# Dilated attention scores of a decoder trunk: from float32 products to float32r parts

## The chip, the cores and the metric

The kernel runs on one core of a Trainium2 chip. The metric is device time in microseconds (us) of one execution, the median of several runs. TensorE (PE in the profile; PEld is its weight load), VectorE (DVE), ScalarE (ACT) and GpSimd (POOL) each work through a queue of their own, in the order in which the program was built; SyncE (SP) issues the transfers. A semaphore makes an instruction at the head of a queue wait for another engine, and everything behind it in that queue waits too.

## The reference, cut to what matters

Two layers; each is a half-step SwiGLU, a token mixing and another half-step SwiGLU, all with residual and layer norm, on 256 tokens of width 1024 in float32. The mixing has 4 MLA heads, 6 dilated heads and 6 NSA heads. The change is in the scores of the dilated heads:

```python
def dilated_attention(q, k, v):
    for window, dil in DIL_PATTERNS:            # (128, 1), (512, 4), (2048, 16)
        o, lse = banded_attention(to_sub(q), to_sub(k), to_sub(v), window // dil)
    ...
    w = jax.nn.softmax(jnp.stack(lses, axis=-1), axis=-1)
    return jnp.einsum('bshp,pbshd->bshd', w, jnp.stack(outs))

o_b = dilated_attention(apply_rope(heads(dq), cos, sin), apply_rope(heads(dk), cos, sin), heads(dv))
```

On 256 tokens the three patterns are one softmax over the causal keys in which every key carries a weight of 0 to 3 (how many patterns reach it), and this is how the kernel computes it.

## The kernel before

Weights are streamed from memory in tiles of 128 x 1024 (`wst`, five buffers). ACT writes a float32r part `wh` of each (L76) and DVE the remainder `wl` (L77); tiles of the next stage's first weights are called `exh` and `exl`. A product of activations and weights is three float32r matmuls (`mm3`, L103 to L105): high by high, high by low, low by high. `ph`, `acc`, `pj` and `acco` are their results in PSUM: SwiGLU in, SwiGLU out, projections of the mixing, and the output projection.

The mixing is written in the order: project `a`, `b`, `nq`, `ks`; MLA; `compressed`; `nsa(0)`; project `dq` and rotate it; `nsa(1)`; project `dk` and rotate it; project `dv`; `dilated(0)`, `dilated(1)`; output projection; layer norm. The index is the block of 128 query tokens. The build's scheduler turns this into one queue for each engine and mixes the stages, so that matmuls of a later stage stand between those of an earlier one.

One unit of attention (`probs`) is: mask and scores on PE into `sc` (L460, L465), row maximum on DVE (L469), exponentials on ACT (L475 for NSA, L477 with a multiplication by the key's weight on DVE, L478, for dilated heads), reciprocal and normalisation on DVE (L480, L486), four transposes on PE into the single PSUM bank `pt` (L490), and a copy to `pT` on ACT (L492). `nsa(1)` has six units. When all units of a block are done, `weigh` multiplies them with the values into `ov` (L502), and `heads_out` (L507 on ACT, L508 on DVE) writes the heads that the output projection reads.

The output projection has 96 matmuls `acco` in a layer, and its eight blocks of heads are taken in the order `O_ORDER = (0, 1, 5, 6, 7, 2, 3, 4)`. Blocks 0 and 1 are MLA, 5 to 7 NSA, 2 to 4 dilated. So 24 matmuls need MLA alone, 18 need `nsa(0)`, 18 need `nsa(1)`, 18 `dilated(0)` and 18 `dilated(1)`: 42 of the 96 can run before `nsa(1)` has ended.

Rotated queries and keys are transposed on PE into the PSUM bank `ptr`, of which there is one (L440). For the dilated heads the copies out of it were, for each block, one of ACT for the queries (L765) and two of ACT for the keys (L773), the latter into a tile with zeros that POOL had set (L769), so that one float32 matmul gives the scores of two heads. The NSA scores already work in float32r parts: queries `nqS` hold the rounded half in partitions 0 to 63 and its remainder in 64 to 127, and keys `ksH`, `ksL` hold each part twice, so that two matmuls give all four products.

Of the kernel before, what the change touches and what calls it, by code (L numbers as in the profile page):

```python
# [49 lines left out]
def trunk(ctx: ExitStack, tc: tile.TileContext, a: dict):  # L50
    nc = tc.nc
# [141 lines left out]
    def cview(c, t, n):  # L193
        return con[:, c + t * n:c + (t + 1) * n]
# [144 lines left out]
    def mixing(l):  # L339
        with tc.tile_pool(name="apool", bufs=1, reuse_waits="tile") as ap_:  # L340
            widths = {"rt1": 384, "rt2": 384, "rq": 384, "qmT": 1024, "kmT": 1536, "wuq": 768, "cT": 768, "pr": 512}

            def new(shape, name, bufs=1, tag=None, dt=F32):

                if tag is None:
                    return ap_.tile(shape, dt, tag=name, name=name, bufs=bufs)
                m = math.prod(shape[1:])
                v = ap_.tile([P, widths.get(tag, 384)], F32, tag=tag, name=name, bufs=bufs)[:shape[0], :m]
                if len(shape) == 3:
                    v = v.rearrange("p (a b) -> p a b", a=shape[1])  # L350
                if len(shape) == 4:
                    v = v.rearrange("p (a b c) -> p a b c", a=shape[1], b=shape[2])
                return v
# [40 lines left out]
            cT = new([P, 3, S], "cT", 1, "cT")  # L394
# [41 lines left out]
            def transposed(src, n, w=P):  # L436

                pv = bank("ptr").rearrange("p (k s) -> p k s", k=4)
                for k in range(n):
                    nc.tensor.transpose(pv[:w, k], src[:, k * w:(k + 1) * w], ident)  # L440
                return pv[:w, :n]

            def rotated(ps, t, H):
                r = new([P, 384], "rq", 2, "rq")
                rope(r[:, :H * 64].rearrange("p (h n) -> p h n", h=H),
                     ps[t][:, :H * 64].rearrange("p (h n) -> p h n", h=H),
                     cview(C_COS, t, 64), cview(C_SIN, t, 64), H, 32)
                return transposed(r, H // 2)
# [69 lines left out]
            for t in range(2):  # L518
# [5 lines left out]
                                     scale=float(128 ** -0.5), accum_out=ss[:, 1:2])  # L524
# [9 lines left out]
                                        in1=gain[:, :, None].to_broadcast([P, 3, P]), op=OP.mult)  # L534
# [4 lines left out]
            qmT = new([96, 4, S], "qmT", 1, "qmT")  # L539
            kmT = new([96, 4, S], "kmT", 1, "kmT")  # L540
            for t in range(2):
                tsl = slice(t * P, (t + 1) * P)
# [24 lines left out]
            for v in range(2):  # L567
                for g in range(2):
                    for par in range(2):
                        src = kcT[g * 64:(g + 1) * 64, v, :].rearrange("p (c j r) -> p j r c", j=8, r=2)  # L570
                        for half in range(2):

                            rows = slice(8 * half, 8 * half + 8)
                            nc.vector.tensor_tensor(
                                out=E[par * 64:(par + 1) * 64, v, rows, g * 16:g * 16 + 15],
                                in0=src[:, :, par, half:half + 15],
                                in1=posT[par * 64:(par + 1) * 64, v, rows, None].to_broadcast([64, 8, 15]),
                                op=OP.add)
# [131 lines left out]
            def dilated(t):  # L710
                tsl = slice(t * P, (t + 1) * P)
                nk = (t + 1) * P
                ov = ov_tile()
                order = in_order()
                neg = tri if t == 0 else dilm
                mult = con[:, C_MULT + 256 - nk:C_MULT + 256]
                pT = {}
                for js in ((0, 1), (2,)) if t == 0 else ((0,), (1,), (2,)):
                    w = probs(t, [(dqT[:, j, tsl], [dkT[:, j, :, :nk]], 2) for j in js], nk, neg, mult=mult)
                    for i, j in enumerate(js):  # L720
                        pT[j] = w[:, 2 * i * (t + 1):2 * (i + 1) * (t + 1)]
# [12 lines left out]
            nqS = new([P, 2, 3, S], "nqS", dt=F32R)  # L734
            ksH = new([P, 2, 2, S], "ksH", dt=F32R)
            ksL = new([P, 2, 2, S], "ksL", dt=F32R)
            for t in range(2):
                tsl = slice(t * P, (t + 1) * P)
                raw = new([P, 384], "raw", 2, "rq")
                nc.scalar.activation(raw, pn[t][:, :384], AF.Copy)  # L740
                nc.scalar.activation(nqT[:, :, tsl], transposed(raw, 3), AF.Copy, scale=0.125)
                pv = rotated(pn, t, 6)
                for g in range(2):
                    top = nqS[0:64, g, :, tsl]
                    nc.scalar.activation(top, pv[g * 64:(g + 1) * 64], AF.Copy, scale=0.125)  # L745
                    nc.vector.scalar_tensor_tensor(out=nqS[64:128, g, :, tsl], in0=pv[g * 64:(g + 1) * 64], scalar=0.125,
                                                   in1=top.bitcast(F32), op0=OP.mult, op1=OP.subtract)
            mla(0)
            pk_, = project("ks")
            mla(1)  # L750
            for t in range(2):
                tsl = slice(t * P, (t + 1) * P)
                pv = rotated(pk_, t, 4)
                for g in range(2):
                    for half in range(2):
                        hi = ksH[half * 64:(half + 1) * 64, g, :, tsl]
                        nc.scalar.activation(hi, pv[g * 64:(g + 1) * 64], AF.Copy)
                        nc.vector.tensor_tensor(out=ksL[half * 64:(half + 1) * 64, g, :, tsl],
                                                in0=pv[g * 64:(g + 1) * 64], in1=hi.bitcast(F32), op=OP.subtract)
            pTc = [compressed(t) for t in range(2)]  # L760
            nsa(0, pTc[0])
            pdq, = project("dq")
            dqT = new([P, 3, S], "dqT", 1, "qmT")
            for t in range(2):
                nc.scalar.activation(dqT[:, :, t * P:(t + 1) * P], rotated(pdq, t, 6), AF.Copy, scale=0.125)  # L765
            nsa(1, pTc[1])
            pdk, = project("dk")
            dkT = new([P, 3, 2, S], "dkT", 1, "kmT")
            nc.gpsimd.memset(dkT, 0.0)  # L769
            for t in range(2):  # L770
                pv = rotated(pdk, t, 6)
                for g in range(2):
                    nc.scalar.activation(dkT[g * 64:(g + 1) * 64, :, g, t * P:(t + 1) * P],  # L773
                                         pv[g * 64:(g + 1) * 64], AF.Copy)
            pdv, = project("dv")
            vd = [new([P, 6, 64], f"vd{t}", 1, f"qm{t}") for t in range(2)]
            for t in range(2):
# [150 lines left out]
```

## Time and profile before

| | before |
|---|---|
| median of 3 runs | 1044.63 us (1043.99 to 1044.65) |
| profiled execution | 1045.1 us |
| its span in the trace | 1042.4 us |
| mean granted TensorE clock | 0.999 |
| PE busy | 1028.8 us (99%) |
| DVE busy | 666.8 us (64%) |
| ACT busy | 509.0 us (49%) |

The span runs from the first to the last instruction; the 2.7 us between it and the execution's time lie around the program. Busy PE time is the union of records that overlap (a matmul's record outlasts the start of the next), so 99% says that PE rarely stood with nothing in it, and what a matmul costs is read from the distance between starts, not from the length of its record. A share over the whole span says little of a stage: the mixing of layer 0 ends at 333 us, that of layer 1 at 848 us, and in these stages the other engines are far busier than on the mean.

### The profile page before, as it was taken

What the parts mean: (1) busy time and instruction counts of PE and PEld (TensorE: products, weight loads), DVE (VectorE), ACT (ScalarE), POOL (GpSimd) and SP (SyncE); (2) the same over time, 40 slices, a digit from 0 to 9 for tenths busy, and PEclk for the clock granted to TensorE, in tenths of its full rate; (3) what the DMA queues carried; (4) which work ended last, traced back from release to release, by engine and by line L of the source; (5) the groups of instructions that cost most, each with busy time, mean ns of one, the idle gap of its engine ahead of it and who ended that gap; (6) DMA issues with size and microseconds to landing.
All of it is one profiled execution on the core that took longest, in us unless ns stands there. A gap on an engine that the chain in (4) does not pass through costs nothing.

```text
span 1042.4 us, 14003 instructions
## 1 busy us (share of the span) xinstructions
PE 1028.8 (99%) x5226; PEld 841.7 (81%) x5226; DVE 666.8 (64%) x1061; ACT 509.0 (49%) x832; POOL 23.2 (2%) x35
## 2 busy tenths in 40 slices
PE   9999999999999999999999999999999999999997
PEld 6888888878877888888888888888888778888885
DVE  6655555875989555555665555567679884555554
ACT  7544444435785344444334444434358844444440
POOL 0000000100000000000000000002000000000000
PEclk9999999999999999999999999999999999999999
DMA  9866657553462555657565665567515544666541
GB/s 343 307 188 185 192 182 246 202 177 108 134 226 87 173 185 183 185 163 229 171 241 163 185 189 188 183 206 267 189 40 175 190 141 148 184 186 192 182 146 41
DMA packets 59540, 190.22 MB, mean 182 GB/s; under 512 B 7120, under 2 KB 8784, under 8 KB 58704
## 3 DMA queue, kind: packets, MB, share of 16 engines
q1 hardware_dynamic: 59184, 189.07, 56.3%
q8 instruction: 41, 0.67, 0.3%
q10 hardware_dynamic: 288, 0.26, 0.1%
q14 instruction: 27, 0.22, 0.1%
HBM read 188.26 MB, written 1.05 MB: 182 GB/s over the span
## 4 chain that ended last, share of the span: by engine, by line
PE 94%; DMA 2%; ACT 2%; DVE 1%; issue 0%; DVEq 0%; ACTq 0%; SPq 0%
PE ph L105 15%; PE ph L104 15%; PE ph L103 15%; PE acc L105 8%; PE acc L104 8%; PE acc L103 8%; PE pj L105 3%; PE pj L103 3%; PE pj L104 3%; PE ov L502 2%; PE ptg L259 2%; DMA exh<-in_w 2%; PE pt L490 2%; PE acco L103 1%; PE ptr L440 1%; PE sc L465 1%
## 5 line engine op out<-in xcount | busy, mean ns | idle before, releaser
L77 DVE TENSOR_TENSOR wl<-wst,wh 128x1024 fp32r<-128x1024 f32 (+3 forms) x316 | 352.7, 1125 | 256.8 <-ACT wh L76 254.0
L76 ACT ACTIVATE wh<-wst 128x1024 fp32r<-128x1024 f32 (+3 forms) x316 | 307.0, 979 | 284.6 <-PE ph L105 175.6
L103 PE MATMUL ph<-wh,xh 128*128 128x512 f32 x640 | 252.4, 395 | 0.0
L104 PE MATMUL ph<-wl,xh 128*128 128x512 f32 x640 | 250.0, 391 | 0.1
L105 PE MATMUL ph<-wh,xl 128*128 128x512 f32 x640 | 250.1, 391 | 0.0
L104 PEld LDWEIGHTS ph<-wl,xh 128*128 128x128 f32 x640 | 120.3, 188 | 25.0 <-DVE wl L153 0.8
L103 PEld LDWEIGHTS ph<-wh,xh 128*128 128x128 f32 x640 | 120.3, 188 | 24.8 <-ACT wh L152 0.7
L105 PEld LDWEIGHTS ph<-wh,xl 128*128 128x128 f32 x640 | 120.1, 188 | 25.0
L105 PE MATMUL acc<-wh,gl 128*128 128x512 f32 x288 | 113.5, 394 | 0.0
L103 PE MATMUL acc<-wh,gh 128*128 128x512 f32 x288 | 112.9, 392 | 0.0
L104 PE MATMUL acc<-wl,gh 128*128 128x512 f32 x288 | 112.8, 392 | 0.0
L103 PE MATMUL pj<-wh,xh 128*128 128x384 f32 (+3 forms) x224 | 77.9, 348 | 0.3
L105 PE MATMUL pj<-wh,xl 128*128 128x384 f32 (+3 forms) x224 | 78.0, 348 | 0.0
L104 PE MATMUL pj<-wl,xh 128*128 128x384 f32 (+3 forms) x224 | 77.3, 345 | 0.0
L250 ACT ACTIVATE sg<-ph 128x256 f32<-128x256 f32 x88 | 33.5, 384 | 74.4 <-PE ph L105 74.4
L104 PEld LDWEIGHTS acc<-wl,gh 128*128 128x128 f32 x288 | 54.1, 188 | 12.2
L103 PEld LDWEIGHTS acc<-wh,gh 128*128 128x128 f32 x288 | 54.1, 188 | 11.6
L105 PEld LDWEIGHTS acc<-wh,gl 128*128 128x128 f32 x288 | 54.1, 188 | 11.0
L252 DVE TENSOR_TENSOR g<-sg,ph 128x256 f32<-128x256 f32 x88 | 36.7, 421 | 34.0 <-ACT sg L250 16.6
L103 PEld LDWEIGHTS pj<-wh,xh 128*128 128x128 f32 x224 | 42.3, 189 | 2.7 <-ACT nqS L745 0.7
L104 PEld LDWEIGHTS pj<-wl,xh 128*128 128x128 f32 x224 | 42.4, 189 | 1.8
L105 PEld LDWEIGHTS pj<-wh,xl 128*128 128x128 f32 x224 | 42.3, 189 | 1.7
(175 smaller groups left out, 1165.2 us busy)
## 6 DMA issues: line engine op xcount, KB each, us to landing
wst<-in_ffin SPq DMA_DIRECT2D x156, 512.0 KB, 4.5
wst<-in_ffout SPq DMA_DIRECT2D x88, 512.0 KB, 3.6
wst<-in_ffin SPq DMA_DIRECT2D x40, 256.0 KB, 5.0
exh<-in_w SPq DMA_DIRECT2D x16, 512.0 KB, 6.2
wst<-in_w_out SPq DMA_DIRECT2D x16, 512.0 KB, 4.5
gb<-in_lngb SPq DMA_DIRECT2D x6, 1024.0 KB, 6.8
wst<-in_w_b SPq DMA_DIRECT2D x16, 256.0 KB, 5.5
wst<-in_w_nq SPq DMA_DIRECT2D x8, 384.0 KB, 4.8
```

The source lines that it names most:

```text
L76: nc.scalar.activation(h[:, c], src[:, c], AF.Copy)
L77: nc.vector.tensor_tensor(out=l[:, c], in0=src[:, c], in1=h[:, c].bitcast(F32), op=OP.subtract)
L103: nc.tensor.matmul(out, lhsT=xh, rhs=wh, start=start, stop=False)
L104: nc.tensor.matmul(out, lhsT=xh, rhs=wl, start=False, stop=False)
L105: nc.tensor.matmul(out, lhsT=xl, rhs=wh, start=False, stop=stop)
L250: nc.scalar.activation(sg, ps[:, :256], AF.Silu)
L252: nc.vector.tensor_tensor(out=g, in0=sg, in1=ps[:, 256:], op=OP.mult)
L259: nc.tensor.transpose(pt[:, k, t], gs[t][:, k * P:(k + 1) * P], ident)
L440: nc.tensor.transpose(pv[:w, k], src[:, k * w:(k + 1) * w], ident)
L465: nc.tensor.matmul(sv[:, i:i + m] if m > 1 else sv[:, i], lhsT=qT, rhs=part, start=False, stop=True, skip_group_check=True)
L490: nc.tensor.transpose(pt[:, b * P:(b + 1) * P], pr[:, b * P:(b + 1) * P], ident)
L502: order(nc.tensor.matmul(out[g * 64:(g + 1) * 64], lhsT=v, rhs=p_, start=i == 0, stop=i == n - 1, skip_group_check=True))
```

## The change

The scores of the dilated heads are computed from float32r parts, as those of NSA were. The queries become `dqS` (rounded half above its remainder, by `stacked`), the keys `dkH` and `dkL`, `dkM` (rounded part and remainder, each written to both halves of the partitions, by `twice`). The remainder of the third head of a half lies in a tile of its own, `dkM`. The tiles take the places of ended ones: `dqS` that of `kmT`, `dkH` that of `nqS`, `dkL` that of `qmT`, `dkM` that of `cT`. The memset of `dkT` goes. `stacked` and `twice` also take over the unchanged NSA steps.

```diff
+            def stacked(dst, pv, tsl):
+                for g in range(2):
+                    top = dst[0:64, g, :, tsl]
+                    nc.scalar.activation(top, pv[g * 64:(g + 1) * 64], AF.Copy, scale=0.125)
+                    nc.vector.scalar_tensor_tensor(out=dst[64:128, g, :, tsl], in0=pv[g * 64:(g + 1) * 64], scalar=0.125,
+                                                   in1=top.bitcast(F32), op0=OP.mult, op1=OP.subtract)
+            def twice(hi, lo, pv, tsl):
+                for g in range(2):
+                    for half in range(2):
+                        rows = slice(half * 64, (half + 1) * 64)
+                        top = hi[rows, g, :, tsl]
+                        nc.scalar.activation(top, pv[g * 64:(g + 1) * 64], AF.Copy)
+                        j = 0
+                        for l in lo:
+                            n = l.shape[2]
+                            nc.vector.tensor_tensor(out=l[rows, g, :, tsl], in0=pv[g * 64:(g + 1) * 64, j:j + n],
+                                                    in1=top[:, j:j + n].bitcast(F32), op=OP.subtract)
+                            j += n
...
-                    w = probs(t, [(dqT[:, j, tsl], [dkT[:, j, :, :nk]], 2) for j in js], nk, neg, mult=mult)
+                    w = probs(t, [(dqS[:, g, j, tsl], [dkH[:, g, j, :nk], dkL[j][:, g, :nk]], 1)
+                                  for j in js for g in range(2)], nk, neg, mult=mult)
...
-            dqT = new([P, 3, S], "dqT", 1, "qmT")
-            for t in range(2):
-                nc.scalar.activation(dqT[:, :, t * P:(t + 1) * P], rotated(pdq, t, 6), AF.Copy, scale=0.125)
+            dqS = new([P, 2, 3, S], "dqS", 1, "kmT", F32R)
+            for t in range(2):
+                stacked(dqS, rotated(pdq, t, 6), slice(t * P, (t + 1) * P))
             nsa(1, pTc[1])
             pdk, = project("dk")
-            dkT = new([P, 3, 2, S], "dkT", 1, "kmT")
-            nc.gpsimd.memset(dkT, 0.0)
-            for t in range(2):
-                pv = rotated(pdk, t, 6)
-                for g in range(2):
-                    nc.scalar.activation(dkT[g * 64:(g + 1) * 64, :, g, t * P:(t + 1) * P],
-                                         pv[g * 64:(g + 1) * 64], AF.Copy)
+            dkH = ap_.tile([P, 2, 3, S], F32R, tag="nqS", name="dkH", bufs=1)
+            dkL01 = new([P, 2, 2, S], "dkL", 1, "qmT", F32R)
+            dkL2 = new([P, 2, 1, S], "dkM", 1, "cT", F32R)
+            dkL = [dkL01[:, :, 0], dkL01[:, :, 1], dkL2[:, :, 0]]
+            for t in range(2):
+                twice(dkH, [dkL01, dkL2], rotated(pdk, t, 6), slice(t * P, (t + 1) * P))
```

The scheduler also lays the queues out anew. Three places are shown; those of layer 1 read the same. In the changed kernel the lines have moved: L743 and L744 are the two instructions of `stacked`, L753 and L757 those of `twice`.

**PE, from the second transposition of the rotated dilated queries into the units of `nsa(1)`.** Before, `ptr` is that transposition, `pt` are the transposes of one unit of `nsa(1)`:

```order
L440 MATMUL ptr<-ident,rq 128x128 x3
L104 MATMUL acco<-wl,oTh 128x512
L105 MATMUL acco<-wh,oTl 128x512
L103 MATMUL acco<-wh,oTh 128x512
L490 MATMUL pt<-ident,pr 128x128 x4
L104 MATMUL acco<-wl,oTh 128x512
L105 MATMUL acco<-wh,oTl 128x512
L103 MATMUL acco<-wh,oTh 128x512
L104 MATMUL acco<-wl,oTh 128x512
L490 MATMUL pt<-ident,pr 128x128 x4
L105 MATMUL acco<-wh,oTl 128x512
```

Of the changed kernel, the end of 18 `acco` that follow the second `ptr`, and all that stands from there to the products `ov` of `nsa(1)`:

```order
L104 MATMUL acco<-wl,oTh 128x512
L105 MATMUL acco<-wh,oTl 128x512
L490 MATMUL pt<-ident,pr 128x128 x8
L460 LDWEIGHTS identb
L460 MATMUL sc<-tri,identb 128x2x128
L465 MATMUL sc<-ksH,nqS 128x512
L465 MATMUL sc<-ksL,nqS 128x512
L490 MATMUL pt<-ident,pr 128x128 x4
L460 LDWEIGHTS identb
L460 MATMUL sc<-tri,identb 128x512
L490 MATMUL pt<-ident,pr 128x128 x4
L460 LDWEIGHTS identb
```

Before, 1 `acco` stands between the two `ptr`, 3 between the second and the first `pt`, and 25 between the first `pt` and `ov`. In the changed kernel these counts are 18, 18 and 0. Later, 43 stand from the end of `nsa(1)`'s `ov` to that of `dilated(1)` before, and 35 in the changed kernel.

**DVE, at the last three units of `nsa(1)`.** Before (`exl` are splits of the first weights of the SwiGLU that follows the mixing; L480, L485 and L486 end a unit):

```order
L469 TENSOR_REDUCE nm<-sc 128x2
L485 TENSOR_TENSOR rs<-rs,gates_1829 128x2
L480 RECIPROCAL rs<-rs 128x2
L486 TENSOR_TENSOR pr<-pr,rs 128x512
L485 TENSOR_TENSOR rs<-rs,gates_1829 128x2
L486 TENSOR_TENSOR pr<-pr,rs 128x512
L77 TENSOR_TENSOR wl<-wst,wh 128x1024
L480 RECIPROCAL rs<-rs 128x2
L485 TENSOR_TENSOR rs<-rs,gates_1829 128x2
L486 TENSOR_TENSOR pr<-pr,rs 128x512
L77 TENSOR_TENSOR wl<-wst,wh 128x1024
L77 TENSOR_TENSOR exl<-wst,exh 128x512 x8
```

In the changed kernel:

```order
L744 SCALAR_TENSOR_TENSOR dqS<-ptr,dqS 64x3x128
L77 TENSOR_TENSOR wl<-wst,wh 128x1024
L744 SCALAR_TENSOR_TENSOR dqS<-ptr,dqS 64x3x128
L77 TENSOR_TENSOR exl<-wst,exh 128x512 x5
L480 RECIPROCAL rs<-rs 128x2
L77 TENSOR_TENSOR exl<-wst,exh 128x512
L485 TENSOR_TENSOR rs<-rs,gates_1829 128x2
L469 TENSOR_REDUCE nm<-sc 128x2
L486 TENSOR_TENSOR pr<-pr,rs 128x512
L480 RECIPROCAL rs<-rs 128x2
L77 TENSOR_TENSOR exl<-wst,exh 128x512
L485 TENSOR_TENSOR rs<-rs,gates_1829 128x2
```

The eight splits `exl` stood behind the last unit of `nsa(1)`; five of them now stand ahead of the last three units and three between these, while the splits `wl` have moved ahead.

**DVE, from the end of `nsa(1)` into the dilated heads.** Before (`nm` is a unit's row maximum, L478 the weighting of its exponentials):

```order
L508 TENSOR_TENSOR oTl<-ov,oTh 128x384
L469 TENSOR_REDUCE nm<-sc 128x4
L469 TENSOR_REDUCE nm<-sc 128x2
L478 SCALAR_TENSOR_TENSOR pr,rs<-pr,con 128x128 x5
L480 RECIPROCAL rs<-rs 128x4
```

In the changed kernel:

```order
L508 TENSOR_TENSOR oTl<-ov,oTh 128x384
L757 TENSOR_TENSOR dkL<-ptr,dkH 64x2x128
L757 TENSOR_TENSOR dkM<-ptr,dkH 64x128
L757 TENSOR_TENSOR dkL<-ptr,dkH 64x2x128
L757 TENSOR_TENSOR dkM<-ptr,dkH 64x128
L77 TENSOR_TENSOR wl<-wst,wh 128x1024
L757 TENSOR_TENSOR dkL<-ptr,dkH 64x2x128
L757 TENSOR_TENSOR dkM<-ptr,dkH 64x128
L77 TENSOR_TENSOR wl<-wst,wh 128x1024
L757 TENSOR_TENSOR dkL<-ptr,dkH 64x2x128
L757 TENSOR_TENSOR dkM<-ptr,dkH 64x128
L77 TENSOR_TENSOR wl<-wst,wh 128x1024
```

Eight pairs of `dkL` and `dkM` now stand between the end of `nsa(1)` and the last unit of `dilated(1)`. On ACT the eight copies `dkH` (L753) stand where four copies `dkT` stood; the first of each block waits for PE's transposes, each of the other three for DVE.

## Rows read from the trace of the kernel before

**Rows 1.** The page, busy time of each engine, with its share and instructions.

```profile
PE 1028.8 (99%) x5226; PEld 841.7 (81%) x5226; DVE 666.8 (64%) x1061; ACT 509.0 (49%) x832; POOL 23.2 (2%) x35
```

**Rows 2.** Busy time by engine in stretches of both layers' mixing.

```profile
core 0: us, PE busy (x) PEld busy (x) DVE busy (x) ACT busy (x) POOL busy (x), PEclk, DMA share, GB/s
291.07:293.34 2.27, 2.27 (x15) 1.65 (x14) 2.27 (x6) 1.45 (x3) 0.00 (x0) 1.00 0.43 120
293.34:303.06 9.72, 9.72 (x55) 7.21 (x54) 9.27 (x19) 9.03 (x23) 0.00 (x0) 1.00 0.59 189
303.06:306.50 3.44, 3.44 (x61) 3.27 (x61) 3.34 (x7) 2.83 (x6) 0.00 (x0) 1.00 0.90 283
306.50:325.74 19.24, 18.74 (x96) 13.34 (x94) 16.25 (x48) 12.40 (x26) 0.00 (x0) 1.00 0.50 164
325.74:333.25 7.51, 6.92 (x50) 5.56 (x51) 6.51 (x13) 2.88 (x5) 0.93 (x1) 1.00 0.04 13
808.19:817.91 9.72, 9.72 (x56) 7.18 (x55) 9.27 (x19) 9.02 (x23) 0.00 (x0) 1.00 0.59 189
821.34:840.58 19.24, 18.74 (x96) 13.34 (x94) 16.25 (x48) 12.40 (x26) 0.00 (x0) 1.00 0.50 160
```

**Rows 3.** Timeline of PE, layer 0: start, length, instruction, idle before it.

```profile
291.07 0.55 PE L440 MATMUL ptr<-ident,rq 128*128 128x128 f32 x3
...
293.34 0.66 PE L490 MATMUL pt<-ident,pr 128*128 128x128 f32 x4
...
294.77 0.60 PE L490 MATMUL pt<-ident,pr 128*128 128x128 f32 x4
...
303.06 1.09 PE L502 MATMUL ov<-pT,vs 128*64 128x128 f32 x16
...
306.50 0.55 PE L440 MATMUL ptr<-ident,rq 128*128 128x128 f32 x3
...
325.74 1.53 PE L502 MATMUL ov<-pT,vd 128*64 128x128 f32 x24 [0.46 <-ACT pT L492]
```

**Rows 4.** The same timeline: first and last of nine `acco` in a row.

```profile
319.12 0.40 PE L105 MATMUL acco<-wh,oTl 128*128 128x512 f32 x1
...
320.99 0.40 PE L104 MATMUL acco<-wl,oTh 128*128 128x512 f32 x1
```

**Rows 5.** The same timeline: dilated scores, each float32 matmul two records, and what follows.

```profile
308.57 1.46 PE L465 MATMUL sc<-dkT,dqT 128*128 128x256 f32 x6
309.68 0.59 PE L104 MATMUL acco<-wl,oTh 128*128 128x512 f32 x1
...
311.83 1.02 PE L465 MATMUL sc<-dkT,dqT 128*128 128x512 f32 x2
312.68 0.38 PE L460 MATMUL sc<-dilm,identb 128*128 128x512 bf16 x1
```

**Rows 6.** The same timeline: first and last of three float32r scores of NSA.

```profile
270.03 0.28 PE L465 MATMUL sc<-ksL,nqS 128*128 128x256 f32 x1
...
270.26 0.28 PE L465 MATMUL sc<-ksL,nqS 128*128 128x256 f32 x1
```

**Rows 7.** Groups by line and shape: count, busy us, mean ns, idle before.

```profile
L773 ACT ACTIVATE dkT<-ptr 64x384 f32<-64x384 f32 x8 | 3.9, 486 | 1.4 <-PE ptr L440 1.3
L765 ACT ACTIVATE dqT<-ptr 128x384 f32<-128x384 f32 x4 | 2.0, 492 | 1.3 <-PE ptr L440 1.3
L746 DVE SCALAR_TENSOR_TENSOR nqS<-ptr,nqS 64x384 fp32r<-64x384 f32 x8 | 4.4, 556 | 1.7 <-ACT nqS L745 1.5
L758 DVE TENSOR_TENSOR ksL<-ptr,ksH 64x256 fp32r<-64x256 f32 x16 | 6.7, 421 | 0.6
L574 DVE TENSOR_TENSOR exl<-kcT,posT 64x120 f32<-64x120 f32 x32 | 7.9, 276 | 0.3
```

**Rows 8.** Waits, whole trace: total us, times, longest.

```profile
ACT ksH L757 <- DVE ksL L758: 2.0, 4, 0.5
```

**Rows 9.** Timeline of DVE, layer 0: the eight splits `exl`.

```profile
301.94 5.09 DVE L77 TENSOR_TENSOR exl<-wst,exh 128x512 fp32r<-128x512 f32 x8
```

**Rows 10.** Timeline of PE: the matmuls that warm it up, at the program's start.

```profile
1.19 4.45 PE L163 MATMUL warm<-zero 128*128 128x512 bf16 x10 [1.19 <-DVE zero L160]
```

More of the change, by code (lines that the diff above doesn't have):

```diff
@@ L347, in new @@
                 m = math.prod(shape[1:])
-                v = ap_.tile([P, widths.get(tag, 384)], F32, tag=tag, name=name, bufs=bufs)[:shape[0], :m]
+                v = ap_.tile([P, widths.get(tag, 384)], dt, tag=tag, name=name, bufs=bufs)[:shape[0], :m]
                 if len(shape) == 3:
@@ L741, in mixing @@
                 nc.scalar.activation(nqT[:, :, tsl], transposed(raw, 3), AF.Copy, scale=0.125)
-                pv = rotated(pn, t, 6)
-                for g in range(2):
[L744 to L747, printed above, removed]
+                stacked(nqS, rotated(pn, t, 6), tsl)
             mla(0)
@@ L752, in mixing @@
                 tsl = slice(t * P, (t + 1) * P)
[L753 to L759, printed above, removed]
+                twice(ksH, [ksL], rotated(pk_, t, 4), tsl)
             pTc = [compressed(t) for t in range(2)]
@@ L762, in mixing @@
             pdq, = project("dq")
-            dqT = new([P, 3, S], "dqT", 1, "qmT")
+            dqS = new([P, 2, 3, S], "dqS", 1, "kmT", F32R)
             for t in range(2):
-                nc.scalar.activation(dqT[:, :, t * P:(t + 1) * P], rotated(pdq, t, 6), AF.Copy, scale=0.125)
+                stacked(dqS, rotated(pdq, t, 6), slice(t * P, (t + 1) * P))
             nsa(1, pTc[1])
             pdk, = project("dk")
-            dkT = new([P, 3, 2, S], "dkT", 1, "kmT")
-            nc.gpsimd.memset(dkT, 0.0)
+            dkH = ap_.tile([P, 2, 3, S], F32R, tag="nqS", name="dkH", bufs=1)
+            dkL01 = new([P, 2, 2, S], "dkL", 1, "qmT", F32R)
+            dkL2 = new([P, 2, 1, S], "dkM", 1, "cT", F32R)
+            dkL = [dkL01[:, :, 0], dkL01[:, :, 1], dkL2[:, :, 0]]
             for t in range(2):
-                pv = rotated(pdk, t, 6)
-                for g in range(2):
-                    nc.scalar.activation(dkT[g * 64:(g + 1) * 64, :, g, t * P:(t + 1) * P],
-                                         pv[g * 64:(g + 1) * 64], AF.Copy)
+                twice(dkH, [dkL01, dkL2], rotated(pdk, t, 6), slice(t * P, (t + 1) * P))
             pdv, = project("dv")
```

## The prediction

> **What bounds the kernel now.** I read the page's shares first: PE is busy 99% of the span, DVE 64%, ACT 49% [rows 1]. By these alone PE is the bound, and each PE cycle saved is time saved. A share over a whole span hides stages, though, so I then read the stage that the change touches. I cut the end of layer 0's mixing at five points of PE's timeline [rows 3]: A, from the first transposition of the rotated dilated queries (291.07) to the first transposes of `nsa(1)` (293.34); B, from there to the first products of `nsa(1)` (303.06); the products themselves, 3.44 us; C, from the first transposition of the dilated keys (306.50) to the products of `dilated(1)` (325.74); D, from there to the SwiGLU (333.25). The busy times of these stretches [rows 2] are to be read across: PE is full, but in B DVE is busy 9.27 and ACT 9.03 of 9.72 us, and in C DVE 16.25 of 19.24. Here three engines are nearly full at once. PE is full only because matmuls of the output projection stand between the steps of the softmax units, 25 of them in B and 43 in C. Layer 1 shows the same lengths, 9.72 and 19.24 [rows 2], so every sum below counts twice.
>
> **The matmuls themselves.** Before, three float32 matmuls of 256 columns take 1.11 us (308.57 to 309.68) and one of 512 takes 0.85 (311.83 to 312.68) [rows 5]: in a layer 1.11 + 3 x 0.85 = 3.7 us. Now there are 12 float32r matmuls of 128 columns and 12 of 256. Those of 256 stand 0.23 / 2 = 0.12 apart for NSA [rows 6], so 1.4 us. No row has one of 128 columns. Below, half of 0.12 bounds it (0.06); above, half of a 256-column float32 matmul (1.11 / 3 / 2 = 0.19). I take 0.11, near the row of the same type, since each still loads 128 columns of weights: 12 x 0.11 = 1.3. So PE saves 3.7 - 2.7 = 1.0 us in a layer, 1.6 or 0.0 at the bounds. This is a gain only where PE sets the pace.
>
> **Stage A, the moved matmuls.** The queue decides. Before, 4 `acco` stand between the first `ptr` and the first `pt` of `nsa(1)`; now 18 + 18 = 36. PE takes its matmuls in order, and one `acco` costs (320.99 - 319.12) / 8 = 0.234 us [rows 4]. The units of `nsa(1)` therefore start 32 x 0.234 = 7.5 us later. Moving work forward on a full engine is free as long as what it leaves behind stays full; that is the question of B. Inside A the new query steps are hidden: for each block ACT does two copies of about 0.49 where it did one of 0.49, and DVE adds two of 0.556 [rows 7], 3.2 us on both engines together in a layer, under 36 x 0.234 = 8.4 us of matmuls. They must alternate (copy, remainder, copy, remainder) before the bank is free for the second `ptr`: 2 x (0.49 + 0.556) = 2.1 us and whatever else stands between them in the two queues; the 18 `acco` there cover 18 x 0.234 = 4.2. If that cover were gone, A would be longer by what exceeds it, at most a few tenths.
>
> **Stage B, the units without cover.** All 42 `acco` that don't need `nsa(1)` are now used up ahead of it, and none stands in B. What is left for PE there is six groups of transposes and three scores. The units wait for ACT and DVE: the bank `pt` is single, so a unit's transposes wait for the copy of the previous one. Two neighbours without exponentials between them stood 1.43 us apart (293.34 to 294.77) [rows 3]; six such rounds are 8.6 us, the lower bound. The exponentials of the last three units stand behind the first copies in ACT's queue, now as before, so these units can't have run ahead during A. On DVE, splits `exl` of 5.09 / 8 = 0.64 us [rows 9] stand among the units where `wl` stood. As a chain of the same length on the same engines I keep B at 9.7 us: 0, or -1.1 at the lower bound. PE's 25 x 0.234 = 5.9 us of cover are gone and B is no shorter, so the 7.5 us of A are lost whole.
>
> **Stage C, the keys.** Before, four copies of 0.486 on ACT brought the keys in. Now there are eight, and sixteen remainders on DVE: 64 x 256 at 0.421, and 64 x 128, which no row has, at the 0.276 of 64 x 120 [rows 7]. That is 8 x 0.697 = 5.6 us on DVE, which was busy 16.25 in C and keeps its units and its three splits `wl` there: 21.8 us. This alone is more than the 19.24 that C took. Besides, each copy after a block's first waits for DVE's remainders. NSA's keys do that now, and the trace shows the wait [rows 8]. In the first steps DVE has nothing else in its queue, so it idles for two copies and their handover, 2 x 0.6 = 1.2 us. C becomes 21.8 + 1.2 = 23.0 us: +3.8. Lower bound +2.6 (no idling). Upper bound: the eight steps, 0.486 + 0.697 each, lie wholly in the chain where four copies lay, 9.5 - 1.9 = +7.6. I take +3.8, since the units of `dilated(0)` and the splits can fill the gaps of the second block. The 1.0 us saved on PE lies in this stage, where DVE now sets the end; it buys nothing. D keeps its work (19 `acco` instead of 18): 0. The memset was on POOL, busy 2% [rows 1]; no engine waits for it: 0.
>
> **The sum.** 7.5 + 0 + 3.8 = 11.3 us in a layer, 22.6 in two. The profiled execution took 1045.1 us, so 1067.7; the median of the runs lies 0.5 lower, so I predict 1067 us, 2.2% more.
>
> **Rivals.** (1) *PE sets the end everywhere*: the shares say so [rows 1], and PE had no idle time in A, B and most of C. Then only its work counts, 2 x 1.0 us less: 1043 us, or between 1041 and 1045 at the bounds of the 128-column price. It needs B to shrink by the full 7.5 us, that is to 2.2, and C not to grow; the two break even when B and C together give back 7.5 us in a layer. Against it: DVE's 9.27 of 9.72 and six rounds of 1.43. Chance 0.07, of which 0.04 faster by over 0.2% (about what a measurement of this kernel can tell from no change) and 0.03 within it. (2) *The units are cheaper without neighbours*: B falls to 8.6 and the keys hide behind the units in C: 7.5 - 1.1 = 6.4 a layer, 1058 us. For it speaks DVE's 3 us of idle time in C. Chance 0.10. (3) *The keys go through in single file*: 7.5 + 7.6 = 15.1 a layer, 1075 us. For it: the bank `ptr` is single, so the second block's transposition waits for the first block's last remainder. Chance 0.10. (4) *The clock falls* while PE waits in B and C. In every stretch read here the granted clock is 1.00, the 2.4 GHz level [rows 2], but in none does PE wait as much as it now would. At the program's start 512 columns took 4.45 / 10 = 0.445 us [rows 10] instead of 0.234; the 54 `acco` after B at that price would add 54 x 0.21 = 11.4 us a layer: 1090 us. The Trainium skill ("TensorE: Matmul & The Clock Gate", Part 1) says that the low level is the default and that activity releases it, which speaks for this rival; no stretch of this trace shows a fall after waiting. PE keeps working about half of B in short pieces, so I give it 0.04.
>
> **How the numbers follow.** The forecast, A and C both paid, has 0.69; its own range, from B and C at their bounds, is 1063 to 1075. With rivals (2) and (3) the range 1057 to 1077 holds about 0.89; what is left out is the clock and rival (1). The likeliest, 1067, is the prediction. Slower by over 0.2%: 0.69 + 0.10 + 0.10 + 0.04 = 0.93; within it 0.03; faster 0.04.
>
> **What would show it.** In the changed kernel's PE timeline the first `pt` of `nsa(1)` should stand about 10 us behind the first dilated `ptr` (2.27 before), with no idle time between. B should be 8.6 to 10.5 us long with PE idle for some 5 of them, waiting for ACT's `pT` and DVE's `pr`. C should be 22 to 24 us, with DVE nearly full and ACT's `dkH` waiting for DVE. The sums of the two layers should agree to some tenths. `sc<-dkH` of 256 columns should stand 0.12 apart. I am wrong if PE shows no idle time there (rival 1: PE reaches the transposes early, or the units ran ahead), wrong in size if C stays at 19 us (the keys hide) or passes 26, and wrong in mechanism if the lost time lies in the SwiGLU stages, which the change should leave as they are.

## The result, and the profile after

The changed kernel takes 1080.66 us (median of 4 runs, 1079.02 to 1081.78) where the kernel before took 1044.64 beside it: a ratio of 1.0345 (95% interval 1.0332 to 1.0358), 36.0 us slower. The forecast was 1067 (1057 to 1077): the sign was right, the size lies outside the range. The profiled execution took 1081.8 us, its span 1079.6; the mean granted clock is 0.978 where it was 0.999.

| layer 0, us | before | forecast | after | layer 1 after |
|---|---|---|---|---|
| A | 2.27 | 9.8 | 10.16 | 10.16 |
| B | 9.72 | 9.7 | 11.45 | 11.25 |
| products `ov` of `nsa(1)` | 3.44 | 3.4 | 6.39 | 5.78 |
| C | 19.24 | 23.0 | 25.41 | 25.14 |
| D | 7.51 | 7.5 | 7.92 | 7.91 |
| sum | 42.18 | 53.5 | 61.33 | 60.24 |

The page's first rows answer to [rows 1]:

```profile
PE 1047.1 (97%) x5250; PEld 858.0 (79%) x5250; DVE 681.9 (63%) x1101; ACT 517.3 (48%) x844; POOL 19.6 (2%) x33
```

DVE has 15.1 us more work, ACT 8.3, PE's records 18.3, although PE was given less to do: its records are longer where the clock is low (below, the same products take 6.39 us instead of 3.44). The stretches A, B, `ov`, C and D of layer 0 and B, `ov` and C of layer 1, the same view as [rows 2]:

```profile
core 0: us, PE busy (x) PEld busy (x) DVE busy (x) ACT busy (x) POOL busy (x), PEclk, DMA share, GB/s
291.15:301.31 10.16, 9.84 (x48) 7.75 (x46) 9.81 (x15) 7.89 (x13) 0.00 (x0) 1.00 0.56 178
301.31:312.76 11.45, 7.11 (x29) 4.41 (x30) 8.05 (x18) 7.24 (x20) 0.00 (x0) 0.67 0.80 254
312.76:319.15 6.39, 6.39 (x60) 6.22 (x61) 0.00 (x0) 0.00 (x0) 0.00 (x0) 0.52 0.01 3
319.15:344.56 25.41, 20.09 (x100) 15.46 (x99) 20.94 (x62) 14.80 (x30) 0.00 (x0) 0.80 0.19 62
344.56:352.48 7.92, 7.46 (x53) 5.65 (x52) 5.86 (x11) 3.04 (x5) 0.93 (x1) 1.00 0.01 4
...
835.24:846.49 11.25, 6.75 (x30) 4.36 (x30) 8.05 (x18) 7.35 (x20) 0.00 (x0) 0.76 0.78 261
846.49:852.27 5.78, 5.78 (x60) 5.61 (x61) 0.00 (x0) 0.00 (x0) 0.00 (x0) 0.58 0.00 1
852.27:877.41 25.14, 19.84 (x101) 15.19 (x99) 20.86 (x62) 14.89 (x30) 0.00 (x0) 0.80 0.21 63
```

Three things are new. In B no engine is full (PE 7.11 of 11.45, DVE 8.05, ACT 7.24): the units wait for each other. The granted clock, 1.00 in every row of before, is 0.67 in B and 0.52 in the products, so most of both ran at the lower level, 1.2 of 2.4 GHz; the same matmuls take 6.39 us instead of 3.44, while ACT and DVE stand still for all of it. And C has PE idle for 5.3 us. PE's timeline, to be held against [rows 3]:

```profile
291.15 0.55 PE L440 MATMUL ptr<-ident,rq 128*128 128x128 f32 x3
...
296.30 0.49 PE L440 MATMUL ptr<-ident,rq 128*128 128x128 f32 x3
...
301.31 0.63 PE L490 MATMUL pt<-ident,pr 128*128 128x128 f32 x4 [0.32 <-DVE dqS L744]
303.87 0.66 PE L490 MATMUL pt<-ident,pr 128*128 128x128 f32 x4 [1.94 <-ACT pT L492]
...
309.18 1.09 PE L490 MATMUL pt<-ident,pr 128*128 128x128 f32 x4
310.96 1.11 PE L490 MATMUL pt<-ident,pr 128*128 128x128 f32 x4 [0.69 <-ACT pT L492]
312.76 1.97 PE L502 MATMUL ov<-pT,vs 128*64 128x128 f32 x16 [0.69 <-ACT pT L492]
...
330.78 0.58 PE L460 MATMUL sc<-dilm,identb 128*128 128x512 bf16 x1 [3.37 <-ACT pr L477]
```

The first `pt` of `nsa(1)`, a softmax unit's transposes, waits for **DVE's `dqS`**, the remainder of the dilated queries. The forecast had no such wait. The code gives the reason: the helper call `bank("ptr")` takes the default tag `"pt"`, so `ptr` and `pt` are one PSUM bank, which the text ahead treats as two. Whoever holds it, a query step or a unit, holds up the other. The second wait, 1.94 us, is explained by ACT's timeline:

```profile
302.57 0.63 ACT L76 ACTIVATE exh<-wst 128x512 fp32r<-128x512 f32 x1 [1.30 <-DMA wst<-in_ffin]
303.22 0.60 ACT L492 ACTIVATE pT<-pt 128x512 f32<-128x512 f32 x1
```

In ACT's queue a split of the SwiGLU's first weights stands ahead of the unit's copy, and its transfer had not landed. The SwiGLU stages themselves kept their lengths: from the end of layer 0's mixing to the first dilated `ptr` of layer 1's it took 472.7 us before and 472.6 after.

### The profile page after: what moved, and what is told of

The parts are those of the page before. It is cut to its first block, busy times and chain, and to the rows that moved or that the text cites. A ratio compares the mean times of both kernels' runs of the same rounds, so it can differ in the third digit from the quotient of the medians.

```text
span 1079.6 us, 14082 instructions
## 1 busy us (share of the span) xinstructions
PE 1047.1 (97%) x5250; PEld 858.0 (79%) x5250; DVE 681.9 (63%) x1101; ACT 517.3 (48%) x844; POOL 19.6 (2%) x33
## 4 chain that ended last, share of the span: by engine, by line
PE 91%; ACT 3%; DMA 3%; DVE 2%; issue 1%; DVEq 0%; ACTq 0%; SPq 0%
PE ph L105 15%; PE ph L104 15%; PE ph L103 15%; PE acc L105 8%; PE acc L104 7%; PE acc L103 7%; PE pj L105 3%; PE pj L103 3%; PE pj L104 3%; PE ov L502 2%; PE ptg L259 2%; PE pt L490 2%; PE sc L465 2%; DMA exh<-in_w 1%; ACT wh L76 1%; PE ptr L440 1%
```

## The experiments

Each kernel ran beside the kernel before; the ratio to it is what compares across calls. The sum is A to D of layer 0, in the trace.

| kernel | us | ratio (95% interval) | sum, us |
|---|---|---|---|
| changed kernel | 1080.66 | 1.0345 (1.0332 to 1.0358) | 61.3 |
| e2_held | 1079.95 | 1.0329 (1.0314 to 1.0344) | 59.5 |
| e1_fill | 1073.59 | 1.0278 (1.0258 to 1.0298) | 57.2 |
| e5_late | 1072.63 | 1.0276 (1.025 to 1.0303) | 55.9 |
| e12_fill_late | 1072.33 | 1.0264 (1.0249 to 1.0279) | 55.1 |
| e3_q | 1072.21 | 1.0263 (1.0246 to 1.028) | 57.8 |
| e4_f32k | 1069.81 | 1.0239 (1.0225 to 1.0253) | 54.3 |
| e3_k | 1069.48 | 1.0235 (1.0217 to 1.0254) | 55.7 |
| e3_both | 1065.80 | 1.0199 (1.0179 to 1.0219) | 52.9 |
| e9_pool | 1065.63 | 1.0185 (1.0166 to 1.0204) | 52.0 |
| e10_own_late | 1063.89 | 1.0179 (1.0164 to 1.0194) | 51.2 |
| e7_own_tile | 1059.99 | 1.0145 (1.013 to 1.016) | 49.8 |
| e6_both_f32k | 1058.52 | 1.0125 (1.0107 to 1.0144) | 49.7 |
| e8_own_tile_f32k | 1056.42 | 1.0109 (1.0094 to 1.0124) | 47.3 |
| e11_own_f32k_late | 1054.99 | 1.0096 (1.0079 to 1.0113) | 47.0 |
| e14_plain_q | 1051.53 | 1.0061 (1.0046 to 1.0077) | 45.7 |
| e15_plain_qk | 1046.95 | 1.0012 (0.9997 to 1.0027) | 43.1 |
| e13_before_late | 1044.21 | 0.9996 (0.9987 to 1.0005) | 41.7 |

**Is A the moved matmuls?** e2_held puts the `acco` back behind the units' transposes, by a dependency that only fixes the order:

```diff
+                    if i < 2 or i < 5 and t == 0:
+                        held.append(r)
+                        n = sum(len(held) > c for c in (10, 14, 15, 21, 26, 30))
+                        if n:
+                            after_it(r, units[n - 1])
```

> The `acco` that do not need `nsa(1)` are held behind its transposes in PE's queue in about the numbers they had before the change (4 in A, about 20 in B, the rest in C). Theory 'the shared bank sets A': `pt` of `nsa(1)` waits for the second block's last remainder, so A stays long without its matmuls, about 6 to 7 us with PE idle for 4, B is about 9.7 again and the clock stays up: 1062 to 1068. Rival 'the order alone is the cause': A is 2.3 to 3.5 and B 9.7 as before, only C stays longer: 1052 to 1058. Third: where the `acco` stand makes no difference to the sum: 1079 to 1082.

The third case came: no difference. A, B and C:

```profile
290.84:298.85 8.01, 2.55 (x15) 1.76 (x14) 7.56 (x14) 4.89 (x9) 0.00 (x0) 0.92 0.41 131
298.85:310.56 11.71, 11.68 (x51) 8.51 (x52) 8.62 (x17) 8.72 (x22) 0.00 (x0) 0.76 0.55 175
...
314.00:342.45 28.45, 23.49 (x111) 18.04 (x109) 21.08 (x62) 14.63 (x30) 0.00 (x0) 0.76 0.27 86
```

and the two waits in A, from PE's timeline:

```profile
294.56 0.52 PE L446 MATMUL ptr<-ident,rq 128*128 128x128 f32 x3 [1.68 <-DVE dqS L753]
298.85 0.88 PE L498 MATMUL pt<-ident,pr 128*128 128x128 f32 x3 [3.77 <-DVE dqS L753]
```

With 4 `acco` instead of 36, A is still 8.01 us, and PE stands idle for 5.5 of it. Of the 7.9 us by which A grew, 5.7 are there without the moved matmuls and 2.2 went with them: the matmuls mostly filled a hole that the bank made. The two blocks held the bank for 3.7 and 4.3 us (290.84 to 294.56 to 298.85). Put back, the matmuls meet a PE whose clock has fallen: B, full of work, takes 11.71 at a mean clock of 0.76, and C, with 45 `acco` instead of 35, takes 28.45.

**Is the clock a cost of its own?** e1_fill adds bf16 matmuls, into a quarter of a bank that nobody reads, where PE waited; e5_late holds the last two of eight `exh` pieces behind `nsa(1)`'s copies on ACT; e12_fill_late does both:

```diff
+            def keep_busy(ov, n, r):
+                for _ in range(n):
+                    f = nc.tensor.matmul(ov[:, 3], lhsT=identb, rhs=tri, start=True, stop=True, skip_group_check=True)
+                    after_it(f, r)
+                    r = f
+                fl.append(r)
+                return r
...
+            r = nc.scalar.activation(h[:, c], src[:, c], AF.Copy)
+            if more and late:
+                skip[0] -= 1
+                if skip[0] < 0:
+                    tc.add_manual_dep(
+                        r.ins, late[-1].ins.name,
+                        mybir.DependencyInfo(mybir.DependencyClass.NoSync, mybir.DependencyReason.DATA),
+                        reason="place in the queue")
...
+            late.append(copies[-1])
+            skip[0] = 6
```

> Added work only: bf16 matmuls of 128 columns into a free quarter of the bank `ov` (30 between the first two units of `nsa(1)`, 16 between the others, 12 ahead of its products, 40 ahead of the first scores of `dilated(1)`), so that PE waits less; the masks of `dilated(0)` come a little later in PE's queue. Theory 'the clock is a cost of its own': no stretch at 0.5 is left from A to C, the products of `nsa(1)` fall from 6.4 back to about 3.5 us, B and C lose about 1 us each, and the time falls by 8 to 14 us, to 1067 to 1073, though PE is given more work. Rival 'the engines' chain sets the end, and the clock is only its symptom': B and C keep their lengths (11.4 and 25.4), 1078 to 1083.

> Of the eight pieces of `exh` that ACT splits ahead of or among the units of `nsa(1)`, the last two are held behind the last `pT` copy of `nsa(1)`, so that ACT's first `pT` no longer stands behind a transfer that lands late. Theory 'the landing costs B its 1.3 us': B falls from 11.4 to 9.7 to 10.3 and the time by 2 to 4 us, to 1077 to 1079. Rival 'the chain of the units sets B whatever is ahead of it': B 11 to 11.5, 1080 to 1082.

> The changed kernel with the added matmuls that keep PE busy and with the last two pieces of `exh` held back. Theory 'clock and landing are two costs': the gains add, 1080.7 - 7.1 - 8.0 = 1065.6, or 1064 to 1068, with the products at 3.4 and B under 9.7. Rival 'one cost seen twice (the wait for the landing lets the clock fall)': no better than the hold alone, 1071 to 1074.

B, the products and C of layer 0 in each of the three, and last the C of layer 1 in e12:

```profile
301.88:312.59 10.71, 9.66 (x133) 8.97 (x133) 8.15 (x18) 7.25 (x20) 0.00 (x0) 1.00 0.79 264
312.59:316.03 3.44, 3.44 (x60) 3.27 (x61) 0.00 (x0) 0.00 (x0) 0.00 (x0) 1.00 0.01 6
316.03:341.03 25.00, 21.21 (x142) 16.68 (x141) 20.99 (x62) 14.69 (x30) 0.00 (x0) 0.93 0.20 64
```

```profile
301.93:310.63 8.70, 4.85 (x30) 3.00 (x30) 6.63 (x16) 6.18 (x19) 0.00 (x0) 1.00 0.83 274
310.63:315.67 5.04, 5.04 (x60) 4.87 (x60) 1.29 (x2) 0.98 (x2) 0.00 (x0) 0.67 0.35 111
315.67:339.79 24.12, 18.57 (x100) 14.22 (x99) 20.82 (x62) 14.82 (x30) 0.00 (x0) 0.86 0.21 66
```

```profile
301.19:311.06 9.87, 9.66 (x133) 8.97 (x133) 7.04 (x16) 6.37 (x20) 0.00 (x0) 1.00 0.72 243
311.06:314.50 3.44, 3.44 (x60) 3.27 (x61) 1.29 (x2) 0.99 (x2) 0.00 (x0) 1.00 0.19 38
314.50:338.19 23.69, 19.89 (x142) 15.59 (x140) 20.83 (x62) 14.79 (x30) 0.00 (x0) 1.00 0.25 84
...
842.87:869.36 26.49, 22.71 (x142) 17.85 (x141) 21.07 (x62) 14.68 (x30) 0.00 (x0) 0.87 0.23 76
```

More work on PE made the kernel 7 us faster, with the clock at 1.00 in B and the products at 3.44 again: the clock is shown to cost, 2.95 us in the products of layer 0 and 2.34 in those of layer 1. C kept its length, but its clock was still 0.93, so e1 can't price the clock there.

Holding two splits back was worth 7 to 8 us, more than the 2 to 4 expected, though one of its five runs stood at 1079.33: B fell to 8.70, close to the forecast's lower bound of six rounds of 1.43, and the clock stayed up to its end.

The two gains do not add (1072.3 instead of 1065.6). In e12 the added matmuls themselves nearly fill B (PE 9.66 of 9.87), so it can't show whether the landing and the clock are one loss or two. Its C shows something else, the price of the clock there: with the same instructions it took 23.69 us in layer 0, at 1.00, and 26.49 in layer 1, where the clock fell (mean 0.87). So the fall cost 2.8 us, and without it e12 would have stood at about 1069.5 (an estimate, 1072.3 less 2.8), still short of the sum of both gains. PE's waits ahead of that place were the same in both layers (0.52, 0.75 and 0.29 us); why the clock fell in only one of them is not shown.

**Is it the bank?** The third kind of experiment lets the bank go at once: one ACT copy of 128x384 per block into SBUF, from which high parts and remainders are then made. e3_both does it for queries and keys, e3_q and e3_k for one of them, in a buffer of the rotation (`rt1`); e7_own_tile in the place of the ended `wuq`:

```diff
+            def out_of_bank(c, t, pv, scale=1.0):
+                nc.scalar.activation(c[:, 3 * t:3 * t + 3], pv, AF.Copy, scale=scale)
+                return c[:, 3 * t:3 * t + 3]
...
-                stacked(dqS, rotated(pdq, t, 6), slice(t * P, (t + 1) * P))
+                stacked(dqS, out_of_bank(cq, t, rotated(pdq, t, 6)), slice(t * P, (t + 1) * P))
```

> One ACT copy of 128x384 per block takes the transposes out of the bank at once, for the dilated queries and the keys; high parts and remainders then read the copy (one ACT operation more per block, 4 in a layer). Theory 'the bank held through four alternating steps is the cause': the order of the `acco` around `nsa(1)` comes back nearly as it was, A is 2.5 to 4, B 9.7 to 10.5, the products 3.4, C 21 to 23, no low clock in A and B: 1050 to 1058. Rival 'the added work of ACT and DVE is the cause': it is all still there and 2 us more in a layer, so 1078 to 1086.

> The same early copy for the dilated queries alone; the keys stay as in the changed kernel. Theory 'the bank': A, B and the products as with both copies, C about 25 as in the changed kernel: 1058 to 1066. Rival 'the added work': 1078 to 1084. The difference to the kernel with both copies is what the keys' hold on the bank costs: 4 to 10 us by the theory.

> The early copy out of the bank for the dilated keys alone; the queries stay as in the changed kernel. If the two copies' gains add, the keys' copy is worth what it was beside the queries' (1072.2 - 1065.8 = 6.4 us): 1073 to 1076, A 10.2, B 11.4 and a slow clock at the products as in the changed kernel, C 21 to 23. Rival 'the keys' cost is DVE's work and not the bank': C 24 to 25.5 and 1079 to 1082.

> The early copies for queries and keys again, but into a tile of their own (the place of the ended `wuq`) instead of the rotation's two temporaries `rt1`, which the second block's rotation needs. Theory 'bank': with nothing else held, A comes back to 3 to 4 (one `acco` stands between the two `ptr`, as before the change), B is 9.7 to 10.7, C 23 to 25 with the keys' remainders still on DVE: 1054 to 1059, which is 7 to 11 under the first pair of copies. Rival 'A is set by ACT's and DVE's added steps, 4 copies and 4 remainders': A stays at 6 to 6.5, 1064 to 1067.

The first pair gained 15 us, not the 23 to 31 expected, and A was 6.38 there. The single copies do not tell queries from keys, either: 8 us for the queries' copy and 11 for the keys' alone make 15 together, and e3_k was faster than both of its cases. In e3_q A, B and the products gave back 8.0 us in layer 0, but C, with 42 `acco` instead of 35, grew from 25.41 to 29.89. e7 differs from e3_both only in the buffer, which the second block's rotation needs in e3: with a tile of its own A is nearly what it was before the change (2.27), and the granted clock is 1.00 all through the mixing. A, B and C of e7_own_tile:

```profile
291.02:293.63 2.61, 2.61 (x16) 1.83 (x15) 2.55 (x5) 2.40 (x6) 0.00 (x0) 1.00 0.55 171
293.63:306.20 12.57, 11.55 (x62) 8.54 (x61) 12.18 (x25) 12.49 (x30) 0.00 (x0) 1.00 0.50 150
...
309.63:333.48 23.85, 17.93 (x102) 13.09 (x100) 21.86 (x65) 15.62 (x32) 0.00 (x0) 1.00 0.38 129
```

More work, four ACT copies a layer, and 21 us less: a ratio of 1.0145 after 1.0345. But C fell by 1.6 us only, no lower than the 23.69 that it took in e12 at a clock of 1.00 with the bank still held: what the keys' hold costs in C beside the clock is not shown. And B is 12.57, where 9.7 to 10.7 was expected, with ACT busy 12.49 and DVE 12.18 of it; that is the next question.

**What the added steps cost.** e4_f32k keeps the doubled keys in float32, so that DVE's 16 remainders fall away and one float32 product per head serves (e6 and e8 with the early copies); e9_pool gives the remainders to POOL; e14_plain_q drops the queries' remainders as well, so that the products are float32 over 64 rows, and e15_plain_qk also the doubling, so that of the change only the early copies and products of one head each are left:

```diff
-            dkH = ap_.tile([P, 2, 3, S], F32R, tag="nqS", name="dkH", bufs=1)
+            dkH = ap_.tile([P, 2, 3, S], F32, tag="nqS", name="dkH", bufs=1)
...
-                    w = probs(t, [(dqS[:, g, j, tsl], [dkH[:, g, j, :nk], dkL[j][:, g, :nk]], 1)
+                    w = probs(t, [(dqS[:, g, j, tsl].bitcast(F32), [dkH[:, g, j, :nk]], 1)
```

Of e9 (where both remainders of a head read the same high part), e14 and e15:

```diff
+                            sub = nc.gpsimd if pool else nc.vector
+                            sub.tensor_tensor(out=l[rows, g, :, tsl], in0=pv[g * 64:(g + 1) * 64, j:j + n],
...
+                    nc.scalar.activation(dqS[0:64, g, :, t * P:(t + 1) * P], pv[g * 64:(g + 1) * 64], AF.Copy, scale=0.125)
...
+                    nc.scalar.activation(dkH[0:64, g, :, t * P:(t + 1) * P], pv[g * 64:(g + 1) * 64], AF.Copy)
```

> The keys' remainders undone: the doubled keys are kept in float32 (eight ACT copies in a layer still, no DVE remainders), and one float32 product per head of the stacked queries takes the place of two float32r products. The queries' side is the changed kernel's. Theory 'the 5.6 us of remainders on DVE lengthen C': C falls from 25.4 to 20 to 21.5, A and B stay: 1070 to 1073. Rival 'the bank, or the eight copies': C stays at 24 to 25.5: 1079 to 1082. By the prediction's own term (C +3.8 of 11.3) it would be 7.6 us in all: 1073.

> The early copies for queries and keys together with the keys in float32. If bank and remainders are separate causes, both gains come: A, B and the products as with the two copies (6.4, 10.7, 3.4), C about 20, D 7.4: 1055 to 1058. If they are one cause seen twice, the time stays near that with the two copies: 1063 to 1067.

> The same with the keys in float32 (no remainders of keys). Theory 'bank and remainders are the whole loss': A 3 to 4, B 9.7 to 10.7, C 19.5 to 20.5: 1044 to 1050, near the kernel before. Rival 'something else is left': over 1053.

> The early copies in their own tile, and the 16 remainders of the keys on POOL instead of DVE; the products are the changed kernel's float32r pairs. Nothing in these traces prices POOL on such an operation; bounds are DVE's 0.28 to 0.42 and, if POOL takes four times as long, 1.1 to 1.7 each. Theory 'DVE is what C lacks': C falls to 20 to 22 if POOL takes up to twice DVE's time, 1046 to 1054. Rival 'the remainders lie on the path to the first scores whoever makes them': C 25 or more: 1058 to 1070.

> From the kernel with own tile and float32 keys: the dilated queries stay float32, too, without a remainder (four DVE operations of 0.56 and nothing else less in a layer), and the products run over 64 rows. Theory 'added steps on ACT and DVE are the rest': B falls by about the 2.2 us of the remainders, from 12.4 to 10 to 10.8, the rest stays (A 2.6, C 21.5): 1051 to 1053. Rival 'the order': B stays over 11.8 and the time at 1055 to 1057.

> The same, and the keys are no longer doubled (four copies of 0.49 on ACT less in a layer). What is left of the change are the four early copies of a layer and products of one head each. Theory 'added steps': C falls to 19.3 to 20.3: 1046 to 1049. Rival 'the order': C stays over 21, 1051 or more.

C of e4_f32k, then B and C of e15_plain_qk, to be read beside the 9.72 and 19.24 of [rows 2]:

```profile
316.90:337.50 20.60, 17.76 (x101) 13.51 (x99) 16.52 (x49) 14.35 (x30) 0.00 (x0) 1.00 0.26 76
```

```profile
293.78:303.36 9.58, 9.58 (x53) 6.80 (x52) 8.25 (x17) 9.54 (x24) 0.00 (x0) 1.00 0.58 183
306.80:325.83 19.03, 19.03 (x103) 13.49 (x101) 16.20 (x48) 13.49 (x28) 0.00 (x0) 1.00 0.44 148
```

With the bank held, dropping the keys' remainders is worth 10.9 us (C 25.41 to 20.60); the clock in C rises from 0.80 to 1.00 with it, so this is not DVE's time alone. With the bank free it is worth 3.6 us only (a ratio of 1.0145 to 1.0109). e6 came at 1058.5, near its case of two separate gains; e8 missed its 1044 to 1050, so bank and key remainders are not the whole loss. Dropping the queries' remainders gives another 4.9, dropping the doubling 4.6; e15 is then within 0.3% of the kernel before, and PE is full in B and C again. Each of these steps also lets the build choose another order (B holds 31 `acco` in e8, 23 in e14), so B and C are read together: 33.9, 32.4, 28.6. POOL does not help; its operations, from the groups by shape:

```profile
L764 POOL TENSOR_TENSOR dkL<-ck,dkH 64x256 fp32r<-64x256 f32 x16 | 11.6, 725 | 202.9 <-PE ptr L440 202.0
L764 POOL TENSOR_TENSOR dkM<-ck,dkH 64x128 fp32r<-64x128 f32 x16 | 7.6, 473 | 0.0
...
L465 PE MATMUL sc<-dkL,dqS 128*128 128x128 f32 x8 | 2.7, 355 | 6.0 <-POOL dkL L764 6.0
```

At 1.7 times DVE's price PE waits 6.0 us for them in the two layers, where in e7, with DVE making them, the same matmuls waited 0.4: on POOL they lie on the path to the first scores. That they would lie there at any price, as the second case says, is not shown.

**Are splits ahead of the copies the rest of B?** e10 and e11 hold seven of the eight `exh` pieces back in e7 and e8 (`skip[0] = 1` in the edit of e5), and e13 does so in the kernel before:

> The copies in their own tile (B 12.6, 1060.0), and seven of the eight `exh` pieces held behind the last `pT` copy of `nsa(1)`. Theory 'splits ahead of the units' copies on ACT': B falls to 9.7 to 10.7, C stays near 23.8 or grows by the pieces that now stand there: 1053 to 1057. Rival 'the four query copies and remainders on ACT and DVE set B': B 12 to 12.6 and 1058 to 1061.

> The same hold in the kernel with the keys in float32 (B 12.6, C 21.5, 1056.4). Theory 'splits': B 9.7 to 10.7: 1049 to 1053, and what is left is C's 2.3 for four more copies. Rival 'added steps': 1054 to 1057.

> The kernel before with seven of the eight pieces held back. PE stands full there, so by the theory the hold buys nothing: 1043 to 1046. If it gains over 2 us, the kernel before had the same wait already, and the hold is no proof for the change.

No. B stayed at 12.2 in both; e10 was even 4 us slower than e7, above both of its cases (C 25.6 instead of 23.85, with the held pieces in it), and e11 about the same as e8. B of e11:

```profile
294.18:306.38 12.20, 11.51 (x61) 8.53 (x61) 10.36 (x21) 9.46 (x24) 0.00 (x0) 1.00 0.47 151
```

ACT is no longer full here (9.46 of 12.20), and B is hardly shorter: the engine nearest to full is PE (11.51). B holds 31 `acco` in e7 to e11 and 25 before the change, which by [rows 4] is 6 x 0.234 = 1.4 of the 2.5 us that it is longer; the rest stays open. In the kernel before, holding the splits back is worth nothing. No version was found that beats the kernel before.

## Why the prediction was wrong, by its steps

Layer 0's sum came 7.8 us over its forecast: 0.4 in A, 1.7 in B, 2.95 in the products, 2.4 in C and 0.4 in D. So the time left the range by the terms of B and the products, put at 0, and by that of C; the step whose mechanism was wrong lies ahead of them.

**The step that failed** is the cover in stage A: "the 18 `acco` there cover 18 x 0.234 = 4.2. If that cover were gone, A would be longer by what exceeds it, at most a few tenths". It rested on 2.1 us per block and on `ptr` and `pt` being two banks. e2_held took that cover away, and A was 5.7 us longer than before the change, not a few tenths: the bank was held 3.7 and 4.3 us per block, since ACT and DVE put splits of 1.2 us, reductions and rotations between the alternating steps, and the units wait for the same bank. A was forecast 7.5 longer and came 7.9 longer, in good part by luck: "the queue decides" holds for 2.2 us of it. In e7, with the same steps and the bank free, A is 2.61.

**Stage B and the products**, forecast at 0, took 1.7 and 2.95 us more in layer 0. Its premise, "a chain of the same length on the same engines", left out that a split waiting for its transfer now stands ahead of the first copy (with two splits held back, B is 8.70). And this is rival (4), put at 0.04: the clock did fall while PE waited. The place and the size were others than it said: not the 54 `acco` after B but the transposes and products at its end, and scores, transposes and products in C. That PE "keeps working about half of B in short pieces" was no argument against it; the clock first fell to the low level after waits of at most 1.94 us, as finer stretches of the changed kernel show (PEclk, first B and the products, then C):

```profile
301.31:305.20 3.89, 1.70 (x11) 1.17 (x11) 3.42 (x7) 2.61 (x8) 0.00 (x0) 1.00 0.83 257
305.20:318.90 13.70, 11.55 (x78) 9.38 (x78) 4.63 (x12) 4.63 (x14) 0.00 (x0) 0.50 0.43 141
319.15:329.10 9.95, 7.10 (x38) 5.52 (x37) 8.03 (x16) 6.71 (x11) 0.00 (x0) 1.00 0.31 95
329.10:339.40 10.30, 7.84 (x35) 5.90 (x35) 8.66 (x37) 5.57 (x15) 0.00 (x0) 0.50 0.18 61
```

PE was busy 1.70 of the 3.89 us before the first fall, 7.10 of 9.95 before the second. The Trainium skill ("TensorE: Matmul & The Clock Gate", A second HAM failure mode: psum-queue depth-cycling) says that short idle times between groups of matmuls, as a kernel cycles through PSUM banks, made the clock of one kernel go up and down. This trace agrees in that the clock fell after waits no longer than 1.94 us, and the section would have given the rival more weight than Part 1 did.

**Stage C** was mis-sized: +3.8 forecast, +6.2 measured, inside its bounds. By its size it is nearer to rival (3), the keys in single file, which had +7.6; but in layer 0 of e12, at a clock of 1.00 and with the keys' steps and the bank as in the changed kernel, C is 23.69, that is +4.5: some 1.7 of the 2.4 us that were missed look to be the clock's. The steps alternate as forecast (`dkH` waits 0.7 us for `dkM`), but the "units of `dilated(0)` and the splits" that were to fill the gaps stand in the same queues and stretch the hold: PE's next scores waited 3.37 us. e4_f32k bears out the remainders as the term's main part: without them C is 20.60.

**Right** were the matmuls' price (0.11 us each of 128 columns at full clock), that PE's saving buys nothing where it lies (PE is idle for 5.3 us of C), D but for 0.4 us, the six rounds of 1.43 as B's floor (8.70 in e5), and that the SwiGLU stages stay.

Divided by the experiments, the 36 us are: about 21 the bank held through alternating steps (changed kernel to e7), with the landing wait and the clock as parts of it, in C perhaps the clock alone; 3.6 the keys' remainders, 4.9 the queries' and 4.6 the doubling once the bank is free; 1 to 2 are left in e15, at the edge of what is measured. The division depends on the order in which things are taken away: the keys' remainders are worth 10.9 when they are taken first, with what the clock gives back then. How much of a step is its own time and how much the order that the build then chooses was not told apart.

## What to carry to other kernels

Before costing work that reads a PSUM bank, look up by its tag who else uses the bank, and count the hold from the transposes to the last reader, with all that stands between the readers in their queues. If two engines must take turns on it, copy it out once: four more copies a layer bought 21 us here. The Trainium skill ("Perfetto Trace Analysis", Optimizing Tensor Performance) asks for independent groups of matmuls to rotate through banks so that emptying one overlaps the next; here the kernel's eight banks (four of accumulators, two of `sc`, one of `pt`, one of `ov`) were all in use, and an early copy into SBUF freed the shared one: A fell from 10.16 to 2.61 us.

Where a scheduler has filled a hole with matmuls, don't price the matmuls: take them out and see whether the hole stays.

## What the runs showed of the hardware

Matmuls that compute nothing made a kernel 7 us faster: with them the granted clock stayed at 1.00 in B and in the products, which gave back 5.3 us in the two layers. In e2_held the clock was low right after a wait of 3.77 us; in the changed kernel it first fell after nothing longer than 1.94 us; in e12 it fell in the C of one layer and not of the other, after the same waits.

Halving the width of a float32r product saves next to nothing: those of 128 columns stand 0.11 us apart in the changed kernel (in a stretch with the clock at 1.00), those of 256 columns 0.12 [rows 6]:

```profile
326.91 0.27 PE L465 MATMUL sc<-dkH,dqS 128*128 128x128 f32 x1
327.02 0.27 PE L465 MATMUL sc<-dkL,dqS 128*128 128x128 f32 x1
327.13 0.28 PE L465 MATMUL sc<-dkM,dqS 128*128 128x128 f32 x1
```

A float32 product of 128 columns costs (316.35 - 315.43) / 4 = 0.23 us in e8, against 0.37 of 256 columns [rows 5]; each is two records:

```profile
315.43 1.16 PE L465 MATMUL sc<-dkH,dqS 128*128 128x128 f32 x8
316.35 0.48 PE L103 MATMUL acco<-wh,oTh 128*128 128x512 f32 x1
```
